# Moving the samples' state update of a state-space mixer to GpSimd, and the causal mask out of TensorE

## The chip, the cores and the metric

The kernel runs on one core of a Trainium2 chip. A core has five engines with instruction queues of their own: TensorE (PE in the profile; its weight loads are PEld), VectorE (DVE), ScalarE (ACT), GpSimd (POOL) and SyncE (SP), which only issues transfers here. The metric is device time in microseconds (us) of one execution of the whole program.

## The reference

One inference step of two layers with 1024 channels, for a prompt of 512 tokens and 8 samples of one token each. Layer 0 uses sparse attention, layer 1 a Mamba-2 mixer, and each is followed by an MLP. The change is in the mixer. For each of 32 heads with state `S` (64 x 128), cut to what matters:

```
xbc = silu(conv(h @ w_xbc));  x, B, C = split(xbc)           # B, C shared by the 8 heads of a group
a_cum  = cumsum(dt * a) within a chunk
decay  = exp(where(l >= s, a_cum[l] - a_cum[s], -1e30))       # causal
y      = ((C B^T) * decay) @ (x * dt)  +  exp(a_cum) * (C @ S_prev)  +  D * x      # prompt
S_new  = exp(dt * a) * S + (x * dt) B^T;   y = S_new C + D * x                     # each sample
out    = rmsnorm(y * silu(z)) @ w_out
```

The sequence result doesn't depend on the chunk length; the kernel uses chunks of 128.

## The kernel before

Activations lie as 128 channels by 520 columns: 512 prompt tokens, then 8 samples. Products with weights are exact to float32 by splitting both sides into a rounded high half and a remainder (float32r): ScalarE copies the high half of a weight tile (`split`, `wh`, line 408) and VectorE subtracts for the low half (line 409), two weights ahead of their product. A product of 128 output channels is 48 matmuls.

The mixer lies between about 890 and 1300 us. Four head groups of four pairs of heads each run through it, in the order of `SSD_SEQ` (line 1942): per pair q the x product of the next pair with its convolution (`ssd_x`), the pair itself (`ssd_pair`), then its z product and gate (`ssd_gate`). At a group's last pair the next group's B and C products come in (`ssd_bc`), at a group's first pair the output product of the group before (`ssd_out`). I call the two pairs of a group that have neither its plain pairs.

In a pair (`ssd_pair`), TensorE spreads the cumulated decay of the two heads over 128 partitions into PSUM (`ps`, line 1512) and adds the causal mask of 0 and -1e30 by a matmul with the identity (line 1514). ScalarE takes the exponential with a bias per chunk (line 1521) into `M`; VectorE multiplies by `cb`, the product of B and C (line 1522). A further spread through `sp` (a GpSimd copy, line 1525, and a matmul, line 1527) gives `E`. `xd` is x times its step, `st` the states from chunk to chunk, `y` the result. For the samples, in each pair, a loop over the 8 samples (lines 1577 to 1582) has ScalarE scale B by x (`xb`), VectorE update the state tile `ss` and VectorE multiply by C with a sum along the free axis (`ys`). The state, 128 x 1024 values, is loaded by SP and stored through GpSimd's queue.

A scheduler orders the instructions of each engine when the program is built, by its own estimate of when operands are ready; on the chip each engine takes its list in that order. So pieces of a pair stand between the matmuls of the neighbouring products. Tile pools set reuse: 4 PSUM tiles `s`, 2 of `M`, 2 of the state `ss`, 3 of `xb`, one `z`, one `y`.

## Time and profile before

| | before |
|---|---|
| median of three runs | 1721.11 us (1719.4 to 1721.38) |
| profiled execution | 1719.56 us, span 1717.9 us |
| PE busy | 1664.7 us (97%) |
| PEld busy | 1538.2 us (90%) |
| DVE busy | 984.0 us (57%) |
| ACT busy | 761.6 us (44%) |
| POOL busy | 143.5 us (8%) |
| mean granted TensorE clock | 0.993 |

The profiled execution's time is its span and what lies around it. Busy shares are means over stages with different limits, so the mixer is read by its own stretches below. Names of buffers come from the program with numbers left out: `a` is the PSUM tile of a product, `s` another PSUM tile, `c` any constant.

### The profile page before, as it was taken

Reading aid. Unit: us, or ns where it says so; the run is one execution under the profiler, and the core shown is the slowest. Engines: PE = TensorE matmul, PEld = TensorE weight load, DVE = VectorE, ACT = ScalarE, POOL = GpSimd, SP = SyncE. Lnnn points to the kernel's source line nnn. Section 1 sums busy time; section 2 is a strip of 40 time slices with the busy share of each in tenths; the row PEclk is TensorE's granted clock in tenths of the full one; section 3 lists DMA queues with packets and bytes.
Section 4 is the critical chain, followed back from the end, with each engine's and each line's share of the span. In section 5 each row is a group of like instructions: output and inputs, shape, how many; then the busy total and the mean of one; then the engine's idle time right before and its main releaser. Section 6 shows DMA issues by size and latency. Waiting matters only on the chain.

```text
span 1717.9 us, 34708 instructions
## 1 busy us (share of the span) xinstructions
PE 1664.7 (97%) x13878; PEld 1538.2 (90%) x13878; DVE 984.0 (57%) x2423; ACT 761.6 (44%) x1624; POOL 143.5 (8%) x303
## 2 busy tenths in 40 slices
PE   7899999999999999999999999999998999999997
PEld 6699877667989999999989898899987999999997
DVE  2543377776464343433478968879797643434344
ACT  3534366666443131322456666646564422323231
POOL 2000112310001000000001102111022000000000
PEclk9999999999999999999999999999999999999999
DMA  8822656545433523333433442344324232323321
GB/s 302 288 87 99 215 195 223 169 148 196 137 126 97 184 87 135 99 135 136 136 135 102 135 166 90 117 135 138 125 89 160 74 99 87 96 90 93 93 86 51
DMA packets 72114, 229.87 MB, mean 134 GB/s; under 512 B 8770, under 2 KB 15218, under 8 KB 71186
## 3 DMA queue, kind: packets, MB, share of 16 engines
q1 hardware_dynamic: 62546, 198.45, 35.1%
q0 software_dynamic: 8832, 28.16, 4.5%
q8 instruction: 109, 1.79, 0.4%
q10 hardware_dynamic: 576, 1.05, 0.2%
q14 instruction: 51, 0.42, 0.1%
HBM read 204.02 MB, written 23.61 MB: 133 GB/s over the span
## 4 chain that ended last, share of the span: by engine, by line
PE 71%; DVE 8%; ACT 2%; issue 1%; POOLq 0%; DMA 0%; SPq 0%; POOL 0%; DVEq 0%; ACTq 0%
PE a L323 60%; PE s L323 5%; PE f L323 2%; PE o L323 1%; DVE wh L336 1%; PE sc L323 1%; PE t L327 1%; DVE c L345 1%; DVE g L345 1%; ACT wh L330 1%; DVE acc L336 1%; PE s L327 0%; DVE ss L1462 0%; PE f L327 0%; ACT h L333 0%
## 5 line engine op out<-in xcount | busy, mean ns | idle before, releaser
L323 PE MATMUL a<-h,wh 128*128 128x256 f32 x5952 | 743.4, 284 | 3.8 <-ACT t L333 1.6
L323 PEld LDWEIGHTS a<-h,wh 128*128 128x128 f32 x5952 | 723.3, 189 | 10.1 <-issue 3.7
L330 ACT ACTIVATE wh<-w 128x1024 fp32r<-128x1024 f32 x212 | 224.5, 1059 | 521.8 <-PE a L323 480.4
L336 DVE TENSOR_TENSOR wh<-w,wh 128x1024 fp32r<-128x1024 f32 x212 | 259.6, 1225 | 266.4 <-ACT wh L330 265.8
L323 PEld LDWEIGHTS a<-hid,wh 128*128 128x128 f32 x3072 | 370.2, 188 | 5.0 <-issue 4.2
L323 PE MATMUL a<-hid,wh 128*128 128x256 f32 (+1 forms) x3072 | 373.7, 283 | 0.0
L336 DVE TENSOR_TENSOR t<-a,c 128x8 f32<-128x8 f32 x72 | 12.0, 167 | 217.4 <-PE a L323 217.4
L323 PE MATMUL a<-yh,wh 128*128 128x256 f32 (+1 forms) x768 | 98.4, 285 | 3.0 <-DVE acc L336 1.5
L323 PEld LDWEIGHTS a<-yh,wh 128*128 128x128 f32 x768 | 93.7, 188 | 5.2 <-DVE acc L336 2.2
L330 ACT ACTIVATE hid<-t 128x520 fp32r<-128x520 f32 x64 | 40.9, 639 | 84.5 <-DVE t L336 84.5
L330 ACT ACTIVATE h<-t 128x128 f32<-128x128 f32 (+3 forms) x128 | 52.5, 440 | 46.5 <-PE t L327 46.3
L333 ACT ACTIVATE h<-sc,m 128x128 f32<-128x128 f32 (+3 forms) x128 | 66.6, 530 | 14.6 <-DVE m L340 12.5
L336 DVE TENSOR_TENSOR hid<-t,hid 128x520 fp32r<-128x520 f32 x64 | 44.7, 700 | 42.3 <-ACT hid L330 42.3
L327 PE MATMUL t<-c,h 128*128 128x128 f32 x320 | 53.5, 281 | 1.9 <-DVE h L340 0.7
L345 DVE SCALAR_TENSOR_TENSOR c<-a,c,c 128x512 f32<-128x512 f32 (+1 forms) x74 | 53.9, 728 | 1.8 <-PE a L323 1.8
L333 ACT ACTIVATE xb<-bc,x 128x128 f32<-128x128 f32 x128 | 46.4, 419 | 15.8 <-DVE xb L345 11.2
L323 PE MATMUL sc<-kv,q 128*128 128x128 f32 (+3 forms) x128 | 49.5, 387 | 0.0
L323 PEld LDWEIGHTS a<-q,wh 128*128 128x128 f32 x384 | 46.3, 188 | 1.0 <-ACT wh L330 0.8
L327 PEld LDWEIGHTS t<-c,h 128*128 128x128 f32 x320 | 34.4, 141 | 13.8 <-issue 7.7
L323 PE MATMUL a<-q,wh 128*128 128x256 f32 (+1 forms) x384 | 46.7, 283 | 0.0
L323 PE MATMUL sc<-kv,c 128*128 128x128 f32 (+3 forms) x128 | 42.3, 331 | 4.2 <-POOL c L947 4.2
L1462 DVE SCALAR_TENSOR_TENSOR ss<-ss,c,xb 128x128 f32<-128x128 f32 x128 | 43.3, 361 | 4.4 <-ACT xb L333 4.2
(366 smaller groups left out, 1941.9 us busy)
## 6 DMA issues: line engine op xcount, KB each, us to landing
w<-in_w_dram SPq DMA_DIRECT2D x128, 512.0 KB, 3.5
w<-in_ada_w_dram SPq DMA_DIRECT2D x80, 512.0 KB, 3.6
w<-in_w_ssd_dram SPq DMA_DIRECT2D x40, 512.0 KB, 3.6
w<-in_w_nsa_dram SPq DMA_DIRECT2D x20, 512.0 KB, 3.6
ss<-in_ssm_dram SPq DMA_DIRECT2D x16, 512.0 KB, 4.3
out_ssm_s_dram<-ss POOLq DMA_DIRECT2D x16, 512.0 KB, 3.0
w<-in_w_sout_dram SPq DMA_DIRECT2D x16, 512.0 KB, 4.1
cm<-in_cmp_dram SPq DMA_DIRECT2D x24, 256.0 KB, 4.0
```

Source lines behind the costliest of these rows:

```text
L323: self.nc.tensor.matmul(out, lhsT, rhs, start=start, stop=stop, skip_group_check=True)
L327: self.nc.tensor.transpose(out, in_, self.C('ident')[0:k, 0:k])
L330: self.nc.scalar.activation(out, in_, AF.Copy, **kw)
L333: self.nc.scalar.activation(out, in_, f, **kw)
L336: self.nc.vector.tensor_tensor(out, a, b, op=op)
L345: self.nc.vector.scalar_tensor_tensor(out, a, s, b, op0=op0, op1=op1, **kw)
L1462: self.nc.vector.scalar_tensor_tensor(out, a, s, b, op0=op0, op1=op1)
```

## The change

The samples' update leaves the loop over samples: four GpSimd operations over 128 x 1024 values (state times decay, B times x, their sum, the result times C) in a function of their own, `ssd_sample`. It is issued behind the gate of the pair before (for the first pair, behind its x product), and the sum over the last axis is taken by VectorE in the gate. There is one `xb` buffer of 128 x 1024 in place of three of 128 x 128. The causal mask becomes a multiplication by 0 and 1 where B and C's product is copied (`cb`), now on VectorE. The exponent is limited to values of 0 and below by a Relu of the negated difference, four per head, followed by one exponential over 512 columns. `E` is taken from `ps` in two halves of 64 partitions, so `sp` and its matmul go. Two small operations of the convolution move from GpSimd to VectorE.

```diff
@@ dt_fin
-        self.ts(self.nac.rearrange(fl), p[:, 0:128], -1.0)
+        self.vcopy(self.ac.rearrange(fl), p[:, 0:128])
@@ conv
-        nc.gpsimd.memset(r[:, 0:3], 0.0)
+        nc.vector.memset(r[:, 0:3], 0.0)
...
-        nc.gpsimd.tensor_copy(self.CP[:, n, :], r[:, 512:515])
+        self.vcopy(self.CP[:, n, :], r[:, 512:515])
@@ ssd_bc
-        self.copy(cb, p)
+        self.tt(cb.rearrange("p (c l) -> p c l", c=4), p.rearrange("p (c l) -> p c l", c=4),
+                self.C('tri')[:, None, :].to_broadcast([128, 4, 128]), ALU.mult)
+    def ssd_sample(self, g, t, G):
+        q = 4 * g + t
+        xs, bc = G['xs'], G['bc']
+        v = self.ssd_state(q)
+        x8 = self.small([128, 8], 'x8', 2)
+        self.tt(x8, xs[:, 2 + t], self.sdb[:, q, 0, :], ALU.mult)
+        sh = [128, 8, 128]
+        x = self.tile('xb', sh)
+        f = self.nc.gpsimd.tensor_tensor
+        f(v, v, self.sdb[:, q, 1, :, None].to_broadcast(sh), op=ALU.mult)
+        f(x, bc[0], x8[:, :, None].to_broadcast(sh), op=ALU.mult)
+        f(v, v, x, op=ALU.add)
+        f(x, v, bc[1], op=ALU.mult)
+        self.store(self.O['ssm_s'][q], v.rearrange("p b n -> p (b n)"))
+        return x
@@ ssd_pair
-            self.mm(ps[e], self.e2R[r, 2 * q + e:2 * q + e + 1].to_broadcast([64, 128]), self.ac2[r], True, False)
-        for e in range(2):
-            self.mm(ps[e].rearrange("p (c l) -> p c l", c=4), self.identR,
-                    self.negsR[:, None, :].to_broadcast([128, 4, 128]), False, True)
+            self.mm(ps[e], self.e2R[r, 2 * q + e:2 * q + e + 1].to_broadcast([64, 128]), self.ac2[r], True, True)
...
-                self.act(m[:, ck(c)], p[:, ck(c)], AF.Exp, bias=self.nac[:, c, h:h + 1])
+                self.act(m[:, ck(c)], p[:, ck(c)], AF.Relu, scale=-1.0, bias=self.ac[:, c, h:h + 1])
+            self.act(m, m, AF.Exp, scale=-1.0)
             self.tt(m, m, cb, ALU.mult)
...
-        sp = self.tile('sp', [64, 2, 64], F32R)
-        self.nc.gpsimd.tensor_copy(sp, self.e2R[0:64, 2 * q:2 * q + 2, None].to_broadcast([64, 2, 64]))
-        p = self.tile('s', [128, 512])
-        self.mm(p[:, 128:512], sp.rearrange("p a b -> p (a b)"), self.ac2[0:64, 128:512], True, True)
         E = self.tile('E', [128, 512])
-        self.act(E[:, 128:512], p[:, 128:512], AF.Exp)
+        for e in range(2):
+            r = slice(64 * e, 64 * e + 64)
+            self.act(E[r, 128:512], ps[e][r, 128:512], AF.Exp)
...
-        for b in range(8):
-            v = w[:, b]
-            x = self.tile('xb', [128, 128])
-            self.act(x, bc[0][:, b], AF.Copy, scale=x8[:, b:b + 1])
-            self.pool_stt(v, v, self.sdb[:, q, 1, b:b + 1], x, ALU.mult, ALU.add)
-            self.stt(x, v, 1.0, bc[1][:, b], ALU.mult, ALU.mult, accum_out=ys[:, b:b + 1])
@@ ssd_gate, behind the z product
+        ys = self.small([128, 8], 'ys', 2)
+        self.nc.vector.tensor_reduce(ys, yn, AX.X, ALU.add)
+        self.stt(y[:, 512:T], xs[:, 2 + t], self.dsk[:, q:q + 1], ys, ALU.mult, ALU.add)
@@ ssd
             elif kind == 'z':
-                self.ssd_gate(g, t, y)
+                self.ssd_gate(g, t, y, G[g]['xs'], Y)
+                if n < 15:
+                    Y = self.ssd_sample((n + 1) // 4, (n + 1) % 4, G[(n + 1) // 4])
```

(`pool_stt` runs on VectorE in spite of its name.) What the scheduler makes of it on GpSimd, in the third group between the additions into `yss` of two plain pairs; `z` and `yss` are the gate's, `cv` is the convolution's input. Before:

```order
L1602 TENSOR_TENSOR yss_11760<-yss_11760,z_14826 128x520
L1525 COPY sp_15106<-c_7410 64x128
L1442 COPY c_7409<-cv_14891 128x3
L1439 MEMSET cv_15327 128x3
L357 DMA out_ssm_p_dram<-st_14958 128x128
L357 DMA out_ssm_s_dram<-ss_14911 128x1024
L1525 COPY sp_15605<-c_7410 64x128
L1602 TENSOR_TENSOR yss_11760<-yss_11760,z_15076 128x520
```

After, the same place:

```order
L1604 TENSOR_TENSOR yss_11728<-yss_11728,z_14533 128x520
L1510 TENSOR_TENSOR ss_15159<-ss_15159,c_11317 128x1024
L1511 TENSOR_TENSOR xb_14768<-bc_13722,x_14766 128x1024
L1512 TENSOR_TENSOR ss_14764<-ss_14764,xb_14768 128x1024
L1513 TENSOR_TENSOR xb_14768<-ss_14764,bc_13722 128x1024
L356 DMA out_ssm_p_dram<-st_14670 128x128
L356 DMA out_ssm_s_dram<-ss_14764 128x1024
L1604 TENSOR_TENSOR yss_11728<-yss_11728,z_14754 128x520
```

Four 128x1024 operations stand where two small copies and a memset stood; the decay product (`ss_15159`) is already that of the pair behind the one whose chain follows it.

VectorE at the same place, before: the end of a pair, with pieces of the samples' loop (`xb`, `ss`) between its steps.

```order
L345 SCALAR_TENSOR_TENSOR xb_15011,ys_14986<-ss_14911,bc_13960 128x128
L336 TENSOR_TENSOR y_14980<-y_14980,E_14935 128x384
L1462 SCALAR_TENSOR_TENSOR ss_14911<-ss_14911,c_11320,xb_15015 128x128
L336 TENSOR_TENSOR x_15159<-xs_13790,c_11320 128x8
L336 TENSOR_TENSOR wh_15200<-w_14771,wh_15199 128x1024
L345 SCALAR_TENSOR_TENSOR xb_15015,ys_14986<-ss_14911,bc_13960 128x128
L345 SCALAR_TENSOR_TENSOR z_15076<-z_15076,a_15027 128x520
L345 SCALAR_TENSOR_TENSOR y_14980<-xs_13790,c_7390,ys_14986 128x8
L336 TENSOR_TENSOR M_15094<-M_15094,g_13946 128x512
L336 TENSOR_TENSOR y_14980<-y_14980,z_15076 128x520
L336 TENSOR_TENSOR M_15100<-M_15100,g_13946 128x512
```

VectorE after, from behind the small product `x_14766` (`x8`) on which GpSimd's `xb_14768` waits, to the sum over it:

```order
L344 SCALAR_TENSOR_TENSOR st_14670<-st_14670,c_99,s_14665 128x64 x6
L344 SCALAR_TENSOR_TENSOR y_14692<-x_14392,c_7387,s_14679 128x512
L335 TENSOR_TENSOR E_14646<-E_14646,s_14688 128x384
L344 SCALAR_TENSOR_TENSOR z_14754<-z_14754,a_14702 128x520
L335 TENSOR_TENSOR y_14692<-y_14692,E_14646 128x384
L335 TENSOR_TENSOR M_14778<-M_14778,g_13708 128x512
L335 TENSOR_TENSOR y_14692<-y_14692,z_14754 128x520
L335 TENSOR_TENSOR xd_14800<-s_14795,c_99 128x512
L335 TENSOR_TENSOR M_14785<-M_14785,g_13708 128x512
L335 TENSOR_TENSOR wh_14846<-w_14475,wh_14845 128x1024
L344 SCALAR_TENSOR_TENSOR yh_14761<-y_14692,c_7384,yh_14760 128x520
L1591 TENSOR_REDUCE ys_15146<-xb_14768 128x8
```

The samples' pieces are gone, and the reduction stands behind GpSimd's chain of the same pair.

## Rows read from the trace of the kernel before

**Rows 1.** Stretches: length; busy PE, PEld, DVE, ACT, POOL; clock; DMA share; GB/s
```profile
1098.74:1142.04 43.30, 42.38 (x339) 39.49 (x339) 32.58 (x91) 23.33 (x65) 3.82 (x8) 1.00 0.39 124
1142.04:1156.45 14.41, 14.41 (x129) 14.12 (x128) 12.85 (x34) 7.24 (x15) 2.74 (x5) 1.00 0.29 86
1156.45:1174.64 18.19, 18.03 (x137) 15.37 (x136) 17.27 (x47) 14.40 (x44) 4.81 (x7) 1.00 0.35 107
1174.64:1203.70 29.06, 28.83 (x247) 28.06 (x246) 25.00 (x71) 16.20 (x36) 3.96 (x9) 1.00 0.47 153
```
**Rows 2.** The same stretches, samples' instructions alone: DVE, ACT busy
```profile
1098.74:1142.04 43.30, 8.69 (x48) 5.79 (x16) 1.00 0.39 124
1142.04:1156.45 14.41, 1.85 (x9) 1.38 (x4) 1.00 0.29 86
1156.45:1174.64 18.19, 3.84 (x16) 2.66 (x7) 1.00 0.35 107
1174.64:1203.70 29.06, 5.17 (x24) 1.78 (x5) 1.00 0.47 153
```
**Rows 3.** Waits of PE, 890 to 1310 us: total, times, longest
```profile
PE a L323 <- DVE acc L336: 1.5, 3, 0.6
```
**Rows 4.** PE in order of time, a pair's masks: start, us
```profile
1157.76 1.16 PE L323 MATMUL s<-c,c 64*128 64x512 f32 x4
1158.85 0.43 PE L323 MATMUL s<-c,sp 64*128 64x384 f32 x1
1159.22 0.66 PE L327 MATMUL s<-c,x 128*128 128x128 f32 x4
```
**Rows 5.** POOL: one line (ns: least/median/largest), then in order of time
```profile
L1602 POOL TENSOR_TENSOR yss<-yss,z x14: 1289/1311/1572, 950.5 to 1279.8; 128x520 f32<-128x520 f32 x14
1101.80 0.28 POOL L1525 CAST sp<-c 64x128 fp32r<-64x128 f32 x1 [1.74 <-PE s L323]
```
**Rows 6.** POOL and DVE in order of time, where they meet
```profile
1159.79 1.21 DVE L336 TENSOR_TENSOR wh<-w,wh 128x1024 fp32r<-128x1024 f32 x1
1159.89 1.16 POOL L1442 COPY c<-cv 128x3 f32<-128x3 f32 x1 [0.17 <-ACT cv L330]
...
1308.58 1.49 POOL L534 TENSOR_TENSOR st<-st,M 128x520 f32<-128x520 f32 x1 [2.13 <-ACT M L333]
1308.82 1.28 DVE L336 TENSOR_TENSOR us<-c,A 128x8 f32<-128x8 f32 x1
1312.10 0.16 DVE L336 TENSOR_TENSOR us<-c,A 128x8 f32<-128x8 f32 x1
```
**Rows 7.** DVE by time, then by line (busy, mean ns), mixer
```profile
1177.97 1.23 DVE L345 SCALAR_TENSOR_TENSOR st<-st,c,s 128x64 f32<-128x64 f32 x6
1179.12 0.74 DVE L345 SCALAR_TENSOR_TENSOR y<-x,c,s 128x512 f32<-128x512 f32 x1
1179.78 0.55 DVE L336 TENSOR_TENSOR E<-E,s 128x384 f32<-128x384 f32 x1
...
L345 DVE SCALAR_TENSOR_TENSOR z<-z,a 128x520 f32<-128x520 f32 x16 | 11.0, 690 | 0.6 <-ACT z L333 0.6
L336 DVE TENSOR_TENSOR y<-y,E 128x384 f32<-128x384 f32 x16 | 8.8, 553 | 0.0
```
**Rows 8.** DVE by line, mixer and the stretch behind it
```profile
L336 DVE TENSOR_TENSOR wh<-w,wh 128x1024 fp32r<-128x1024 f32 x53 | 64.7, 1221 | 28.9 <-ACT wh L330 28.5
...
L495 DVE TENSOR_REDUCE c<-s 128x36 f32<-128x144 f32 x1 | 0.3, 307 | 0.2 <-PE s L327 0.2
```
**Rows 9.** ACT by line, mixer
```profile
L333 ACT ACTIVATE xb<-bc,x 128x128 f32<-128x128 f32 x128 | 46.4, 419 | 15.8 <-DVE xb L345 11.2 <-DVE x L336 3.9 <-DMA bc<-dr 0.5
L333 ACT ACTIVATE th<-x 128x512 f32<-128x512 f32 x16 | 10.3, 642 | 12.2 <-DVE x L345 12.1
```
**Rows 10.** Stretches behind the mixer, columns as in rows 1
```profile
1320.00:1325.00 5.00, 0.95 (x6) 0.29 (x3) 4.93 (x10) 1.90 (x5) 3.08 (x2) 0.99 0.99 391
1325.00:1330.00 5.00, 4.42 (x21) 4.33 (x22) 0.28 (x2) 2.16 (x4) 0.00 (x0) 0.50 0.06 24
```

More of the change, by code (lines that the diff above doesn't have):

```diff
@@ L47, in shape_constants @@
     put('tri', (i[:, None] <= i[None, :]).astype(np.float32))
-    put('negs', np.where(i[:, None] <= i[None, :], 0.0, NEG))
     t = np.arange(4)[None, :, None] * 128 + i[:, None, None]
@@ L1407, in dt_fin @@
         m = self.m[0].rearrange("p a b -> p (a b)")
-        self.nac, self.cd, self.dtde = (m[:, ck(n)].rearrange("p (c h) -> p c h", c=4) for n in range(3))
+        self.ac, self.cd, self.dtde = (m[:, ck(n)].rearrange("p (c h) -> p c h", c=4) for n in range(3))
         fl = "p c h -> p (c h)"
-        self.ts(self.nac.rearrange(fl), p[:, 0:128], -1.0)
+        self.vcopy(self.ac.rearrange(fl), p[:, 0:128])
         self.copy(ae, p[:, 128:256])
@@ L1501, in ssd_state, with ssd_pair @@
         return w
-    def ssd_pair(self, g, t, X, G, w):
+    def ssd_sample(self, g, t, G):
         q = 4 * g + t
-        C, cb, bt, xs, bc = (G[k] for k in ('C', 'cb', 'bt', 'xs', 'bc'))
+        xs, bc = G['xs'], G['bc']
[11 more added lines that the diff above has]
+        return x
+    def ssd_pair(self, g, t, X, G):
+        q = 4 * g + t
+        C, cb, bt, xs = (G[k] for k in ('C', 'cb', 'bt', 'xs'))
         M = []
@@ L1572, in ssd_pair, with ssd_gate @@
         self.tt(y[:, 128:512], y[:, 128:512], E[:, 128:512], ALU.add)
-        x8 = self.small([128, 8], 'x8', 2)
-        self.tt(x8, xs[:, 2 + t], self.sdb[:, q, 0, :], ALU.mult)
-        ys = self.small([128, 8], 'ys', 2)
-        for b in range(8):
-            v = w[:, b]
-            x = self.tile('xb', [128, 128])
-            self.act(x, bc[0][:, b], AF.Copy, scale=x8[:, b:b + 1])
-            self.pool_stt(v, v, self.sdb[:, q, 1, b:b + 1], x, ALU.mult, ALU.add)
-            self.stt(x, v, 1.0, bc[1][:, b], ALU.mult, ALU.mult, accum_out=ys[:, b:b + 1])
-        self.store(self.O['ssm_s'][q], w.rearrange("p b n -> p (b n)"))
-        self.stt(y[:, 512:T], xs[:, 2 + t], self.dsk[:, q:q + 1], ys, ALU.mult, ALU.add)
         return y
-    def ssd_gate(self, g, t, y):
+    def ssd_gate(self, g, t, y, xs, yn):
         q = 4 * g + t
         ps = self.product(('w_ssd', 10 * g + 3 + 2 * t), self.h)
+        ys = self.small([128, 8], 'ys', 2)
+        self.nc.vector.tensor_reduce(ys, yn, AX.X, ALU.add)
+        self.stt(y[:, 512:T], xs[:, 2 + t], self.dsk[:, q:q + 1], ys, ALU.mult, ALU.add)
         z = self.U('z')
```

13 lines of the change are left out of this document (6 added, 7 removed).

## The prediction

> **What bounds the kernel now.** I read four views in turn. First the busy time by stretch, cut at the ends of the pairs of one head group in the mixer [rows 1]. Each stretch runs from one addition into `yss` (end of a gate) to the next. In the two plain pairs (14.41 and 18.19 us, one x and one z product each) TensorE is busy throughout: 14.41 and 18.03 us. So TensorE sets the pace. VectorE is close behind: 12.85 of 14.41, then 17.27 of 18.19 us. In the pair that also makes the next B and C (29.06 us) and in the one that also runs the output product (43.30 us) VectorE has 4 and 11 us free. Second, the same stretches for the samples' work alone [rows 2]: 1.85 and 3.84 us of VectorE in the plain pairs, 5.17 and 8.69 us in the others. The scheduler has put most of that work where VectorE has room. Third, TensorE's waits [rows 3]: the largest sum in the whole mixer is 1.5 us, for VectorE. Fourth, the POOL and DVE rows in order of time [rows 6], for what happens when the two engines meet; the sum hangs on it.
>
> **TensorE.** Per pair the change takes away two mask matmuls and the `sp` matmul. The four 512-column matmuls start at 1157.76 and the `sp` matmul at 1158.85 [rows 4]: 1.09 us, 0.27 each, so 0.54 for two. The next matmuls start 0.37 us after `sp`. Together 0.91 us a pair, 14.6 us for 16 pairs. TensorE is the bound, so this is gained wherever it stays the bound.
>
> **ScalarE.** It loses eight scalings of `xb` a pair (0.42 us each) and gains two exponentials of 512 columns (the 512-column Tanh, 0.64, is the nearest row) and a second half of `E` [rows 9]. It gets lighter, and it is busy 7.24 of 14.41 and 14.40 of 18.19 us in the plain pairs [rows 1], so this hides. The first masked product comes 0.64 us later in a pair; between nothing and 16 times that, 10 us, I take nothing, because in [rows 1] ScalarE's and VectorE's other work decides when that product starts.
>
> **VectorE's own work.** The samples' part [rows 2] goes. What is left of the two plain pairs is 30.12 less 5.69, 24.43 us, 12.2 each. A sum over 1024 elements is added: a reduction of 144 elements took 0.31 and a 1024-column subtraction 1.22 us [rows 8]; between them I take 1.2, since the second has the size. The small memset and copy that leave POOL cost some 0.2. So 13.6 us a plain pair, against 16.3 on average before: free of POOL, VectorE would be well off the path.
>
> **What a POOL operation costs.** Four per pair, 128x1024. The nearest row is the 128x520 addition, 1.31 us (least 1.29) [rows 5]. In proportion that is 2.6 us; with a fixed part of some 0.2 (all of the one-input cast of 128 elements is 0.28 [rows 5]), 2.4. Below stands that cast, whose 0.1 us beyond the fixed part would give about 1.0 for 1024 elements. I take 2.4, by the addition, which is the same operation. The Trainium skill (GPSIMD Engine Reference, section 3.1, Elementwise) gives 4497 ns for 2048 elements; an estimate from it is 2.25 us here, and with it the forecast below would be 1743.
>
> **Where the two meet.** At 1308.58 POOL starts an addition that ends at 1310.07. A VectorE product of only 8 columns, issued at 1308.82, ends at 1310.10: 1.28 us, where the same form alone takes 0.16. The other way round, POOL's copy of three elements takes 1.16 us when a 1.21 us VectorE subtraction runs [rows 6]. So a VectorE instruction with both inputs in SBUF and a POOL instruction that reads SBUF exclude each other for their whole length. Before, POOL ran one such addition a pair. Now it runs five.
>
> I follow one plain pair in the changed order of VectorE with these lengths. The decay product on POOL stands behind `yss`; VectorE's next two-input instruction is at its door at once and waits 2.4. The product `xb` starts behind VectorE's small `x8`; VectorE now has six `st` steps, `y`, `E` and `z`, each with one input in PSUM: 1.15, 0.66, 0.47 and some 0.65 us, 2.9 in all [rows 7], so nothing is lost. `y` plus `E` is ready 2.9 us in, the second POOL operation ends at 4.8: wait 1.9. It runs 0.5 [rows 7], POOL's third operation takes the port, and the product M waits 2.4 behind it. Sum 6.7 us a pair; I take 6.6 because something of the first wait is over by the time VectorE comes. The bounds are 0 (all four under one-input work or idle time) and 9.6 (four times 2.4). The Trainium skill (SBUF — State Buffer, "Who interferes with whom") lets an instruction with one SBUF input and a reduction pass beside POOL; no row here shows one that starts inside a POOL operation, and if they waited too, the upper bound would hold, about 1771.
>
> **The sum, against the profiled execution's 1719.6 (span 1717.9 and 1.7 around it).** Plain pair: 13.6 + 6.6 = 20.2 us of VectorE, against 15.4 (16.3 less 0.9) of TensorE. VectorE is in order, prepares the low half of every weight and the M, `xd` and `st` that TensorE takes a few tenths later, so TensorE waits: 20.2 - 16.3 = +3.9 us. There are eight such pairs: +31.2. The pair with B and C: 19.8 (25.00 less 5.17), 1.2, 0.6 for the memsets and copies, 0.7 for the mask product, 6.6: 28.9 us against 29.06 before, -0.2, three times. The pair with the output product: 23.9 + 8 is far below 43, so TensorE's 0.9 is gained, three times: -2.7. First and last pair: -1.8. Sum 31.2 - 0.6 - 2.7 - 1.8 = +26 us, 1745.7. The median of the runs shown is 1.5 above the profiled time, so 1747.
>
> The state's load moves ahead on SP (0.3 us to issue); it needs the buffer of two pairs ago, whose store stands directly behind that pair's last POOL operation, a pair earlier, so it does not hold the weights behind it. On POOL the store of `ssm_p` and `yss` now stand behind up to four long operations; their readers are a pair away.
>
> **Rivals.**
> - *Hidden.* POOL's operations cost VectorE only idle or one-input time (or cost 1.0 us each: the walk then loses 2.0, and 15.6 us is TensorE's own pace). Then only TensorE's saving is left: 1721.1 - 14.6 = 1706.5. For it: VectorE loses 19.6 us of its own work in each group (the four of [rows 2]), more than the 16 us or so of waits that I add outside the first operation of a pair. Against it: [rows 6], and two plain pairs a group with 3 us of room.
> - *Half hidden.* Half of the 6.6: 16.9 against 16.3, +0.6 in eight pairs, less 6: about 1720.
> - *Every wait reaches TensorE.* In the other pairs too TensorE takes M, `xd` and `st` the moment they exist, and a 2.4 us wait there is not caught up by later room. 64 operations at 1.65 less 14.6: +91, 1812. It decides if TensorE comes to each of the pair's matmuls with no product matmuls left to put ahead of them. Against it: in those pairs VectorE has 4 and 11 us free [rows 1], and there it can be ahead with the weights.
> - *The clock.* After 1320 to 1325, with TensorE busy 0.95 of 5 us, the granted clock was 0.50, the lower level, for the next five [rows 10]. If the waits in the plain pairs open a gap like that, a quarter of 8 times 15.4 us at the lower level adds 31: 1778. In the forecast single waits stay at 2.4 us, so I think it less likely.
>
> **How the numbers follow.** Forecast 0.50 (own range 1730 to 1768), hidden 0.25, half hidden 0.06, every wait 0.12, clock 0.07. The measurement tells apart about 0.2% (3.4 us): faster 0.25, same 0.06, slower 0.69. The range reaches from the hidden case to beyond the clock's, 1705 to 1790; what it leaves is most of "every wait" and the lower edge of "hidden".
>
> **What would show it.** Right: POOL's 128x1024 operations at 2.4 us or above, 64 of them; the mean of `y` plus `E` and of M well above their 0.55 and 0.68 us; plain pairs from `yss` to `yss` near 20 us; TensorE's waits on `wh`, M or `xd` of VectorE summing to some 30 us or more. Wrong: plain pairs near 15.4 us with few waits (hidden), POOL's operations near 1 us, or granted clock below 1.00 inside the mixer. The one term that could sink the forecast is the 6.6 us: should VectorE run into POOL only while it had nothing urgent, the sign turns.

## The result and the profile after

The changed kernel takes 1775.5 us (median of four runs, 1766.1 to 1782.2) against 1721.2 (four runs, 1719.4 to 1729.0): ratio 1.0303, 95% interval 1.0245 to 1.0360. The forecast was 1747. It is slower, as forecast, by about twice the amount. The profiled execution, the fastest of the four, took 1766.1 us (span 1764.5, granted clock 0.980) against 1719.6, +46.6.

First the busy time of the group that [rows 1] shows: the pair with the output product, two plain pairs, the pair with B and C.

```profile
1121.63:1168.39 46.76, 42.12 (x319) 40.31 (x318) 31.63 (x45) 17.24 (x40) 20.67 (x13) 0.93 0.32 107
1168.39:1188.65 20.26, 20.21 (x166) 18.73 (x165) 15.38 (x30) 11.78 (x28) 10.59 (x6) 1.00 0.23 75
1188.65:1208.39 19.74, 16.07 (x107) 13.59 (x106) 17.36 (x33) 13.57 (x40) 10.95 (x8) 0.91 0.30 106
1208.39:1238.58 30.19, 29.94 (x247) 28.39 (x246) 24.69 (x57) 14.90 (x30) 6.96 (x5) 1.00 0.44 145
```

The group took 116.95 us against 104.96. TensorE now stands still in the first and third pair, and the clock, 1.00 before in all four, is below it in just those. Over the whole program: the first addition into `yss` comes 12.7 us later than before, the stretch of the 14 additions is 362.2 us instead of 329.3 (+32.9), the rest +0.9. By kind of pair, against before: seven plain pairs +18.4, three with the output product +11.2, three with B and C +3.3.

TensorE's waits, the answer to [rows 3] (total, times, longest):

```profile
PE s L322 <- DVE xd L335: 23.6, 8, 4.9
PE a L322 <- DVE acc L335: 5.1, 2, 2.6
PE s L322 <- DVE M L335: 2.2, 2, 1.6
```

Next POOL's and VectorE's groups by line (busy, mean ns, idle before and its ends), the answer to [rows 5, 7, 8]:

```profile
L1512 POOL TENSOR_TENSOR ss<-ss,xb 128x1024 f32<-128x1024 f32 x16 | 43.6, 2728 | 1.0
L1513 POOL TENSOR_TENSOR xb<-ss,bc 128x1024 f32<-128x1024 f32 x16 | 41.6, 2600 | 1.2
L1511 POOL TENSOR_TENSOR xb<-bc,x 128x1024 f32<-128x1024 f32 x16 | 32.0, 2001 | 74.5 <-DMA bc<-dr 45.4 <-DVE x L335 26.1 <-DVE ys L1591 1.8
L1510 POOL TENSOR_TENSOR ss<-ss,c 128x1024 f32<-128x1024 f32 x16 | 30.9, 1934 | 88.3 <-DMA ss<-in_ssm_dram 63.9 <-ACT c L329 24.4
...
L335 DVE TENSOR_TENSOR wh<-w,wh 128x1024 fp32r<-128x1024 f32 x52 | 79.7, 1533 | 27.6 <-ACT wh L329 27.5
L1591 DVE TENSOR_REDUCE ys<-xb 128x8 f32<-128x1024 f32 x16 | 19.4, 1211 | 16.1 <-POOL xb L1513 16.1
L335 DVE TENSOR_TENSOR y<-y,E 128x384 f32<-128x384 f32 x15 | 17.5, 1165 | 0.0
L347 DVE COPY c<-cv 128x3 f32<-128x3 f32 x24 | 11.9, 495 | 0.0
L344 DVE SCALAR_TENSOR_TENSOR z<-z,a 128x520 f32<-128x520 f32 x15 | 10.3, 689 | 0.1
```

`wh` (1221 before) and `y` plus `E` (553) are longer, `z`, with one input in PSUM, is not (690). I call the four operations of a pair its chain. Two entries were in no part of the forecast: the reduction waits 16.1 us for POOL's last operation, and POOL's second operation waits 45.4 us for the transfer of B and C. It also waits 26.1 us for VectorE's `x8` (`x` in the row), which the forecast had early. So a chain that is issued a pair ahead does not run a whole pair ahead.

In order of time, all in the group above: the head of the pair with the output product (1119.69 to 1127.38), its middle (to 1150.92), and behind the last "..." the end of the first plain pair:

```profile
1119.69 1.98 POOL L1511 TENSOR_TENSOR xb<-bc,x 128x1024 f32<-128x1024 f32 x1 [20.27 <-DMA bc<-dr]
...
1123.35 3.36 POOL L1512 TENSOR_TENSOR ss<-ss,xb 128x1024 f32<-128x1024 f32 x1
1124.48 2.26 DVE L347 COPY c<-cv 128x3 f32<-128x3 f32 x1
1126.65 0.68 DVE L335 TENSOR_TENSOR xd<-s,c 128x512 f32<-128x512 f32 x1
1127.38 1.72 PE L322 MATMUL s<-xd,g 128*128 128x128 f32 x8 [2.01 <-DVE xd L335]
...
1140.89 1.89 POOL L1511 TENSOR_TENSOR xb<-bc,x 128x1024 f32<-128x1024 f32 x1 [2.69 <-DVE x L335]
1145.67 3.24 POOL L1513 TENSOR_TENSOR xb<-ss,bc 128x1024 f32<-128x1024 f32 x1
1148.95 1.22 DVE L1591 TENSOR_REDUCE ys<-xb 128x8 f32<-128x1024 f32 x1 [2.27 <-POOL xb L1513]
1150.92 1.45 PE L322 MATMUL a<-yh,wh 128*128 128x256 f32 x8 [2.60 <-DVE acc L335]
...
1179.54 0.16 DVE L335 TENSOR_TENSOR x<-xs,c 128x8 f32<-128x8 f32 x1
1179.80 2.18 POOL L1511 TENSOR_TENSOR xb<-bc,x 128x1024 f32<-128x1024 f32 x1 [0.80 <-DVE x L335]
1185.38 2.73 POOL L1513 TENSOR_TENSOR xb<-ss,bc 128x1024 f32<-128x1024 f32 x1
1188.15 1.22 DVE L1591 TENSOR_REDUCE ys<-xb 128x8 f32<-128x1024 f32 x1 [2.28 <-POOL xb L1513]
1191.98 0.68 DVE L335 TENSOR_TENSOR xd<-s,c 128x512 f32<-128x512 f32 x1
1192.72 1.01 PE L322 MATMUL s<-xd,g 128*128 128x128 f32 x3 [3.56 <-DVE xd L335]
```

The group's first chain is held back by B and C, so its tail falls on the head of the pair with the output product; there it holds a three-column copy and with it `xd` and TensorE. The second chain goes on only at 1140.89, 11.7 us behind the end of the first, when VectorE has come to its `x8`; its reduction, already in VectorE's list ahead of the output product's additions, waits for it, and TensorE waits for those. In the plain pair the third chain goes on only at 1179.80, when VectorE has come to `x8`, which stands behind the six `st` steps and `E` there; it ends at 1188.1, the reduction is late, and so are the gate, `xd` behind it, and TensorE by 3.56 us. The order of VectorE shown ahead of the prediction is that of the second plain pair, where `x8` stands ahead of the `st` steps and the reduction does not wait.

Behind most such gaps the clock falls: between 880 and 1330 us TensorE has nine gaps of 2.0 to 4.9 us, and the granted clock drops to 0.50, the lower of its two levels, for some us, during or behind eight of them. Stretches around the gap that ends at 1150.92:

```profile
1148.50:1151.00 2.50, 0.08 (x1) 0.12 (x2) 2.05 (x3) 0.68 (x1) 0.94 (x2) 1.00 0.81 328
1151.00:1153.50 2.50, 2.50 (x15) 2.50 (x16) 1.51 (x2) 0.00 (x0) 0.00 (x0) 0.64 0.28 87
1153.50:1156.00 2.50, 2.50 (x16) 2.50 (x16) 0.38 (x1) 0.00 (x0) 0.28 (x1) 0.68 0.89 311
```

TensorE, busy 0.08 of 2.5 us, is granted 0.64 and 0.68 on average in the next five, though it is busy throughout: 1.7 us of full-speed time not granted.

### The profile page after: what moved, and what is told of

It is laid out like the page before. It is cut to its first block, busy times and chain, and to the rows that moved or that the text cites. A ratio compares the mean times of both kernels' runs of the same rounds, so it can differ in the third digit from the quotient of the medians.

```text
span 1764.5 us, 34107 instructions
## 1 busy us (share of the span) xinstructions
PE 1680.1 (95%) x13830; PEld 1551.3 (88%) x13830; DVE 996.6 (56%) x2106; ACT 746.7 (42%) x1540; POOL 271.6 (15%) x302
## 4 chain that ended last, share of the span: by engine, by line
PE 64%; DVE 11%; ACT 3%; issue 2%; POOL 2%; SPq 1%; POOLq 0%; DMA 0%; DVEq 0%; ACTq 0%
PE a L322 55%; PE s L322 3%; DVE wh L335 2%; PE f L322 1%; PE o L322 1%; DVE x L344 1%; PE sc L322 1%; DVE y L335 1%; PE t L326 1%; DVE c L344 1%; POOL ss L1512 1%; POOL xb L1513 1%; DVE acc L335 1%; ACT wh L329 1%; DVE c L347 1%
## 5 line engine op out<-in xcount | busy, mean ns | idle before, releaser
L322 PE MATMUL a<-h,wh 128*128 128x256 f32 x5952 | 757.4, 286 | 3.9 <-ACT t L332 1.6
L322 PEld LDWEIGHTS a<-h,wh 128*128 128x128 f32 x5952 | 730.9, 190 | 15.9 <-issue 9.2
L335 DVE TENSOR_TENSOR wh<-w,wh 128x1024 fp32r<-128x1024 f32 x212 | 275.7, 1301 | 266.8 <-ACT wh L329 265.1
L322 PE MATMUL a<-yh,wh 128*128 128x256 f32 (+1 forms) x768 | 105.5, 296 | 6.2 <-DVE acc L335 5.1
L322 PEld LDWEIGHTS a<-yh,wh 128*128 128x128 f32 x768 | 99.7, 199 | 9.8 <-issue 8.4
L332 ACT ACTIVATE h<-sc,m 128x128 f32<-128x128 f32 (+3 forms) x128 | 66.6, 530 | 14.5 <-DVE m L339 12.4
L322 PE MATMUL a<-q,wh 128*128 128x256 f32 (+1 forms) x384 | 46.5, 283 | 0.0
L344 DVE SCALAR_TENSOR_TENSOR x<-cv,c,x 128x512 f32<-128x512 f32 x48 | 45.8, 954 | 0.0
```

Of the source, the lines that this page charges most:

```text
L322: self.nc.tensor.matmul(out, lhsT, rhs, start=start, stop=stop, skip_group_check=True)
L332: self.nc.scalar.activation(out, in_, f, **kw)
L335: self.nc.vector.tensor_tensor(out, a, b, op=op)
L344: self.nc.vector.scalar_tensor_tensor(out, a, s, b, op0=op0, op1=op1, **kw)
```

## The experiments

Each time is the ratio to the kernel before, run on the same chip, with its 95% interval. Every edit changes operand times, so the scheduler also writes the lists anew; no run here changes an instruction and leaves all else in place.

**Without POOL's operations.** The state is stored and summed as loaded (the samples' update is left out):

```diff
-        f(v, v, self.sdb[:, q, 1, :, None].to_broadcast(sh), op=ALU.mult)
...
-        f(x, v, bc[1], op=ALU.mult)
-        return x
+        return v
```

> The changed kernel without POOL's four operations a pair (it leaves out the samples' state update: the state is stored as it was loaded and the reduction is taken over it). Everything else of the change stays: order, masks, reduction, copies on VectorE. Theory 1 (POOL's operations and the waits they cause are the whole loss): TensorE's saving is left, about 1705 us, clock 1.00 in the mixer, plain pairs near 15.4 us. Rival 2 (order, Relu under the exponential, or the wait of the reduction cost the time): 1740 to 1775.

0.9954 (0.9922 to 0.9985). The four operations, with the waits for them, are all of the loss: 1.0303 to 0.9954 is 60 us by the medians, 52 by the profiled spans (1764.5 and 1712.2). But only about 8 us of the 14.6 that TensorE saves come out (3 to 13 by the interval), and the plain pairs last 18.06 and 17.02 us, not the 15.4 expected. The first three pairs of the same group:

```profile
1093.54:1134.19 40.65, 40.05 (x327) 37.93 (x326) 24.73 (x43) 15.88 (x35) 2.43 (x4) 1.00 0.34 105
1134.19:1152.25 18.06, 17.46 (x137) 15.35 (x136) 14.48 (x31) 11.63 (x31) 2.40 (x4) 1.00 0.34 113
1152.25:1169.27 17.02, 17.02 (x136) 15.26 (x135) 15.37 (x34) 15.73 (x43) 2.41 (x4) 1.00 0.38 128
```

**The same operations with results that nobody reads** (update left out):

```diff
-        f(v, v, self.sdb[:, q, 1, :, None].to_broadcast(sh), op=ALU.mult)
+        f(x, v, self.sdb[:, q, 1, :, None].to_broadcast(sh), op=ALU.mult)
...
-        return x
+        return v
```

> The changed kernel with the same four POOL operations of the same sizes and operands in SBUF, but their results go to a scratch tile that nobody reads: the reduction is taken over the state as loaded, and the state is stored as loaded (the samples' update is left out of the result). So POOL is as busy as in the changed kernel, and no instruction of VectorE depends on it through these data. Theory 1 (the engines exclude each other at SBUF): the loss stays, 1762 to 1776, at most 8 to 10 us less, for the waits of the reduction on POOL ahead of the additions of the output product (2.3 to 2.6 us, three times) and in the start. Rival (VectorE waits in order for POOL's chain of four, a plain dependency): about 1714, as without POOL's operations.

1.0382 (1.0313 to 1.0451): in its trace no VectorE instruction waits for POOL's results, and it is no faster than the change (14 us slower by the ratios, the intervals overlap). So exclusion alone is enough for the loss. That nothing was gained where the waits of the reduction went, 8 to 10 us by the expectation, is a miss; VectorE's busy time rose by another 25 us (table below), since the operations now meet other instructions. The same run shows what passes: a reduction inside a POOL operation.

```profile
933.67 2.23 POOL L1511 TENSOR_TENSOR xb<-bc,x 128x1024 f32<-128x1024 f32 x1
934.07 1.21 DVE L1591 TENSOR_REDUCE ys<-ss 128x8 f32<-128x1024 f32 x1
```

**Eight halves instead of four operations:**

```diff
-        f(v, v, self.sdb[:, q, 1, :, None].to_broadcast(sh), op=ALU.mult)
+        hs = [slice(0, 4), slice(4, 8)]
+        sh = [128, 4, 128]
+        for s in hs:
+            f(v[:, s], v[:, s], self.sdb[:, q, 1, s, None].to_broadcast(sh), op=ALU.mult)
...
```

> The changed kernel, but each of POOL's four 128x1024 operations in two halves of 128x512, eight a pair. POOL's own time goes up by a fixed part each (some 0.2 us, four times a pair). If the price is set by the total time that POOL holds VectorE (theory 1): the sum of both engines' work is unchanged or some 0.8 us a pair longer, so 1775 to 1788. If it is set by the length of a single wait, with the gaps of TensorE of over 2 us and the clock that falls behind them (theory 1b): the single waits fall to about 1.2 us, VectorE gets in between, the granted clock of the mixer returns towards 1.00 (0.96 in the changed kernel) and the time falls to 1745 to 1765.

1.0314 (1.0253 to 1.0375), and 0.95 of clock in the mixer: halving POOL's operations brings nothing. VectorE was indeed held up 18 us less than in the changed kernel, but its reductions now waited 36.5 us for POOL instead of 16.1.

**The three-column copy on ScalarE, and a reduction of nothing** (the second leaves out the sum over the state):

```diff
-        self.vcopy(self.CP[:, n, :], r[:, 512:515])
+        self.copy(self.CP[:, n, :], r[:, 512:515])
```

> The changed kernel, but the 128x3 copy out of `cv` goes to ScalarE instead of VectorE (the memset stays on VectorE). The trace of the changed kernel shows this copy at 0.5 us on average and up to 2.3 us beside POOL's long operations, directly ahead of the `xd` product that TensorE then waits for 2 to 5 us. Theory 1a (this copy is one of the mis-sized terms): VectorE is freed of 24 times 0.5 us and TensorE of some of its waits on `xd`, so 5 to 15 us less than the changed kernel, 1760 to 1770. Rival (it only stands in front of the same wait: the next instruction with both inputs in SBUF meets the same POOL operation): no difference that can be measured from the changed kernel, 1775.

1.0263 (1.0206 to 1.0319): 7 us less by the ratios, between the two expectations, and the intervals overlap, so the time does not decide. The profile speaks for the rival: without the 24 copies (11.9 us) VectorE is busy 355.3 us from 880 us to the last addition into `yss`, with them 354.7, so other instructions were held up in their place.

```diff
-        self.nc.vector.tensor_reduce(ys, yn, AX.X, ALU.add)
+        self.vcopy(ys, yn[:, :, 0])
```

> The changed kernel with the reduction over 1024 elements replaced by a copy of eight of them (the sum over a sample's state is left out): the dependency on POOL's chain stays, VectorE's 1.2 us a pair go. Theory 1 with VectorE as the bound in the plain pairs: 1.1 us in each of seven plain pairs and about as much in the start, 8 to 12 us less than the changed kernel, about 1763 to 1767. Rival (the price lies in where VectorE meets POOL, not in how much it has to do): within 4 us of the changed kernel, 1772 to 1779.

1.0218 (1.0156 to 1.0279): 15 us less than the change by the ratios, for 16 times 1.1 us less of VectorE's work. It suggests that the price lies also in how much VectorE has to do, almost one for one; the intervals overlap a little, so it is not shown.

**Which chains?** Chains left out by pair (their update is left out), five runs; in place of `q < 2` the others have `q >= 4 and t in (0, 1)`, then `(2, 3)`, `(0,)` and `(1,)`:

```diff
+        if q < 2:
+            self.store(self.O['ssm_s'][q], v.rearrange("p b n -> p (b n)"))
+            return v
```

> The changed kernel without POOL's four operations for samples of the first two pairs only (their state is stored as it was loaded). In the changed kernel the first pair ends 12.7 us later than before, where -0.9 was forecast; two chains of four operations run there one behind the other. Theory 1c (this start is a mis-sized term of its own): 10 to 15 us less than the changed kernel, 1760 to 1766, and the rest of the mixer unchanged. Rival (the start is late for another reason, the later first M or the state's load): less than 4 us gained.

1.0178 (1.0107 to 1.0249): by the ratios 22 us less, more than the 10 to 15 expected; the profiled span is 16.4 us shorter, 14.5 of it before the first addition into `yss`.

> The changed kernel without POOL's four operations for the first and second pair of head groups 2 to 4 (6 of 16 pairs; their samples' state is stored as loaded, so the samples' update of those pairs is left out). In the trace of the changed kernel these two chains run, but for the tail of the second and the head of the first, inside the pair that also has the output product. The reading of the traces so far: that pair carries as much of the loss as the plain ones (46.7 us against 40.7 without any POOL operation), so 15 to 20 us less than the changed kernel, about 1757. The prediction as it stood (that pair has 11 us of VectorE free and hides everything): no more than 3 us less, 1772 to 1776.

1.0118 (1.0068 to 1.0167): 32 us less, twice what I expected.

> The changed kernel without POOL's four operations for the third and fourth pair of head groups 2 to 4 (6 of 16 pairs; their samples' update is left out). Their chains run, but for one operation, inside the two plain pairs. The prediction as it stood (all of the loss is in the plain pairs, +3.9 us over before in each, 4.8 over TensorE's own time): 6 times 4.8, some 27 to 30 us less than the changed kernel, about 1747. The reading of the traces so far (plain pairs 2.2 and 2.7 us longer than without POOL's operations, some of it given back in the next pair): 10 to 15 us less, about 1762.

1.0257 (1.0207 to 1.0307): 8 us, not to be told from the change. So leaving out the chains that run in the plain pairs, on which the forecast stood, gains next to nothing. That is a net result: in the profile the plain pairs of the group are 3.0 and 1.7 us shorter (17.28 and 18.05 us), but the pair with the output product is 3.4 longer (50.16), and reductions wait 8.2 us for POOL in it (2.3 in the change). What these chains cost by themselves is better seen from the run with five left out below.

> The changed kernel without POOL's four operations for the first pair of head groups 2 to 4 (3 of 16 pairs; their samples' update is left out). This chain is held back by the transfer of B and C and runs at the head of the pair with the output product, where TensorE waits 2.0 us for `xd`. If the first chain carries the loss of that pair: most of the 31 us that both chains gave, 1745 to 1755. If it is the second chain: 1765 to 1775. If either alone is enough to spoil the pair: both runs gain less than 10 us.

1.0091 (1.0054 to 1.0127): leaving out the three first chains of groups 2 to 4 gives 36 us by the ratios, all that both had given and more than I expected (24 by the profiled spans). The group then, 106.74 us:

```profile
1116.70:1157.32 40.62, 39.74 (x326) 37.85 (x325) 27.08 (x43) 15.83 (x35) 10.92 (x7) 1.00 0.33 105
1157.32:1176.40 19.08, 18.75 (x149) 16.68 (x148) 15.88 (x31) 11.64 (x31) 9.08 (x7) 1.00 0.22 76
1176.40:1194.25 17.85, 16.48 (x127) 14.30 (x125) 15.20 (x33) 15.96 (x43) 9.62 (x8) 1.00 0.44 144
1194.25:1223.44 29.19, 28.10 (x238) 27.13 (x237) 26.89 (x57) 14.54 (x30) 5.61 (x4) 1.00 0.50 162
```

> The changed kernel without POOL's four operations for the second pair of head groups 2 to 4 (3 of 16 pairs; their samples' update is left out). This chain runs in the middle of the pair with the output product; the reduction of the first pair and the additions of the output product stand behind its operations on VectorE, and TensorE waits 2.6 us for the additions. If the second chain carries the loss: 1745 to 1755; if the first: 1765 to 1775; if either alone is enough: both gain less than 10 us.

1.0237 (1.0184 to 1.0289): 11 us, and the interval overlaps with the change's. So the loss of this pair goes with the first chain, which spoils its own pair's head. But VectorE's list differs too. With the first chain left out, the `x8` of the second stands 9.2 us into the pair with the output product, ahead of the `st` steps (1125.88 us); in the changed kernel it stands 19.0 us into it, behind them (1140.64), and in the first plain pair it moves likewise (9.1 against 11.2). How much of the gain is the chain and how much the new order, no run here separates.

**Five at once** (the update of the first two pairs of the mixer and of the first pair of groups 2 to 4 is left out):

```diff
+        if q in (0, 1, 4, 8, 12):
+            self.store(self.O['ssm_s'][q], v.rearrange("p b n -> p (b n)"))
+            return v
```

> The changed kernel without POOL's four operations for five of the 16 pairs: the first two of the mixer and the first of head groups 2 to 4 (their samples' update is left out); eleven chains run as in the changed kernel. If these five carry the loss and the other eleven fit beside VectorE's work: as without any POOL operation, or a little above, 1713 to 1727 on the scale of before at 1721. If the eleven others have a price as the prediction gave the plain pairs (3.9 us and more each in seven pairs): 1740 or above.

1.0009 (0.9980 to 1.0039), clock 1.00 through the mixer. By the ratios five chains cost 51 us and the other eleven about 9; by the profiled spans 40 and 12. In the plain pair of this run that begins at 1140.10 the chain goes on 9.3 us into the pair (11.4 in the changed kernel, 1179.80 above), is through in 6.9 us (8.3), and the reduction does not wait. Here too `x8` has moved ahead of the `st` steps:

```profile
1149.17 0.17 DVE L335 TENSOR_TENSOR x<-xs,c 128x8 f32<-128x8 f32 x1
1149.41 1.90 POOL L1514 TENSOR_TENSOR xb<-bc,x 128x1024 f32<-128x1024 f32 x1 [8.00 <-DVE x L335]
1150.40 1.24 DVE L344 SCALAR_TENSOR_TENSOR st<-st,c,s 128x64 f32<-128x64 f32 x6 [1.06 <-ACT st L329]
1151.39 2.40 POOL L1515 TENSOR_TENSOR ss<-ss,xb 128x1024 f32<-128x1024 f32 x1
1153.86 2.40 POOL L1516 TENSOR_TENSOR xb<-ss,bc 128x1024 f32<-128x1024 f32 x1
1154.35 2.33 DVE L335 TENSOR_TENSOR y<-y,E 128x384 f32<-128x384 f32 x1
1158.35 1.21 DVE L1594 TENSOR_REDUCE ys<-xb 128x8 f32<-128x1024 f32 x1
```

One of the three operations meets an instruction with two inputs in SBUF (2.33 instead of 0.55 us).

**The five done as before, eleven on POOL** (the result is kept):

```diff
+        w = self.ssd_state(q) if q in (0, 1, 4, 8, 12) else None
...
+        if w is not None:
+            for b in range(8):
+                self.act(x, bc[0][:, b], AF.Copy, scale=x8[:, b:b + 1])
```

> The changed kernel with the samples' update of those five pairs done as before (ScalarE scales, VectorE updates, inside the pair) and of the other eleven on POOL a pair ahead; the result is kept. If the five carry the loss and the work put back finds room as it did before: 1716 to 1728, no different from before. If VectorE's work put back into the pair with the output product and the start costs what it did not cost before (0.6 us of it a pair came to 10 us in the run with one head's clamp): 1735 to 1750.

1.0209 (1.0136 to 1.0282). A miss: the eleven chains are those of the run before, and yet reductions wait 12.4 us for POOL again and TensorE 23.6 us for `xd`. In the first plain pair of the group, which begins at 1165.23:

```profile
1174.33 0.16 DVE L335 TENSOR_TENSOR x<-xs,c 128x8 f32<-128x8 f32 x1
1182.59 1.22 DVE L1607 TENSOR_REDUCE ys<-xb 128x8 f32<-128x1024 f32 x1 [4.14 <-POOL xb L1515]
```

`x8` comes as early as in the run before (9.1 us into the pair), but it stands behind the `st` steps and `E` again, and the reduction stands directly behind `z`, so VectorE has little left to do while the chain runs. Why the order comes out so is not shown.

**The mask part alone, in four versions.** First as it is in the change, the samples' loop as before:

```diff
-            self.act(m[:, ck(c)], p[:, ck(c)], AF.Exp, bias=self.nac[:, c, h:h + 1])
+            self.act(m[:, ck(c)], p[:, ck(c)], AF.Relu, scale=-1.0, bias=self.ac[:, c, h:h + 1])
+        self.act(m, m, AF.Exp, scale=-1.0)
```

> Only the mask part of the change: the causal mask as a product with B.C, Relu under the exponential, E taken from the two heads' own rows, so per pair two 512-column mask matmuls and the `sp` matmul gone; the samples' update stays on VectorE and ScalarE inside the pair and the three-column copies stay on POOL, as before. Theory 1 (the loss of the change is POOL's and VectorE's mutual exclusion alone): TensorE's 0.91 us a pair is gained, 16 times, so about 1706 us, and the granted clock in the mixer stays at 1.00. Rival 2 (the longer chain to the first M, Relu then Exp then product, is what makes TensorE wait in the changed kernel): no gain, or slower than before, 1721 to 1760. Rival 3 (TensorE's saving only turns into waits on VectorE, which is close behind in the plain pairs): about 1713 to 1721.

1.0008 (0.9974 to 1.0042): no gain, Rival 2 or 3. TensorE's matmuls did go, as these rows of before and of this run show for 14 pairs (23.1 to 9.5 us, 0.97 a pair):

```profile
L323 PE MATMUL s<-c,c 64*128 64x512 f32 (+1 forms) x56 | 17.0, 473 | 0.0
L323 PE MATMUL s<-c,sp 64*128 64x384 f32 x14 | 6.1, 436 | 0.0
```

```profile
L322 PE MATMUL s<-c,c 64*128 64x512 f32 x28 | 9.5, 496 | 0.0
```

The same run's ScalarE by line:

```profile
L332 ACT ACTIVATE M<-M 128x512 f32<-128x512 f32 x28 | 17.9, 639 | 0.0
L332 ACT ACTIVATE E<-s 64x384 f32<-64x384 f32 x28 | 13.7, 489 | 0.3
```

Twice 0.64 a pair for the new exponential and twice 0.49 for `E` where one of 0.54 stood: ScalarE has 1.7 us a pair more.

One exponential, no Relu (the decay inside a chunk is left out):

```diff
-                self.act(m[:, ck(c)], p[:, ck(c)], AF.Relu, scale=-1.0, bias=self.ac[:, c, h:h + 1])
-            self.act(m, m, AF.Exp, scale=-1.0)
+                self.act(m[:, ck(c)], p[:, ck(c)], AF.Exp, scale=1e-6, bias=self.ac[:, c, h:h + 1])
```

> The mask part alone (as in the first run of this study) with the two steps of Relu and exponential made one: four exponentials with a bias of a scaled input per head, no 512-column exponential behind them (the decay inside a chunk is left out of the result). Theory A (the 14.6 us of TensorE's matmuls were lost because ScalarE got 1.3 us a pair more and the first M comes later): the saving appears, 1706 to 1712. Theory B (the saving goes into TensorE's waits for VectorE, `xd` and the additions, which set the pace a little behind it): as the mask part alone, 1718 to 1727.

0.9939 (0.9914 to 0.9965): 10.5 us of the 14.6. Theory A: the two exponentials on ScalarE held the saving back, by their load or by the longer way to M; this run takes away both. Then the clamp on VectorE, for one head and for both (the result is kept):

```diff
+                self.ts(m[:, ck(c)], p[:, ck(c)], self.ac[:, c, h:h + 1], 0.0, ALU.subtract, ALU.min)
```

> The mask part alone, with the clamp of the first head's exponents moved from ScalarE (four Relu of 0.38 us) to VectorE (four subtract-and-min steps that read PSUM, some 0.2 us each); the second head's stay on ScalarE. The result is kept. If ScalarE's way to M is what held the saving back: ScalarE loses 1.5 us a pair and VectorE gains 0.8, so part of the 10 us that one exponential gave, 1711 to 1718. If VectorE is as near the bound as ScalarE: no gain, 1718 to 1726.

> As the run before with the clamp of both heads on VectorE: ScalarE loses 3 us a pair against the mask part alone, VectorE gains 1.7. If ScalarE's way to M alone decides: 1706 to 1714, the fastest. If VectorE, at 274 of 328 us in the mixer before this, becomes what TensorE waits for: 1720 to 1735.

1.0057 (1.0028 to 1.0086) and 1.0161 (1.0121 to 1.0201), both above what either expectation allowed. The second is clearly slower than with Relu on ScalarE; the first's interval overlaps with that run's. A step took 0.34 us, not 0.2, so VectorE got 1.2 and 2.4 us a pair more, 19 and 39 in all; the time rose by 8 and 26 us although ScalarE lost as much (its 38.6 us of Relu became 19.0, then none). So VectorE's load weighs more than ScalarE's. The way to M is hardly shorter in these two (four steps of 0.34 us in place of 0.38), so they say nothing of its length.

**The mask part with the eight scalings on POOL** in one operation a pair (the result is kept):

```diff
-            self.act(x, bc[0][:, b], AF.Copy, scale=x8[:, b:b + 1])
+        nc.gpsimd.tensor_tensor(xs8, bc[0], x8[:, :, None].to_broadcast([128, 8, 128]), op=ALU.mult)
```

> The mask part alone, and of the samples' update only the eight scalings of `xb` a pair moved from ScalarE to one broadcast multiplication of 128x1024 on POOL; state update and products with C stay on VectorE inside the pair. One long POOL operation a pair instead of four. If the loss goes with POOL's time beside VectorE (1.9 of the 9 us of the four, 52 us in all): some 11 us above the mask part alone, 1732 to 1738, less what ScalarE's 3.4 us a pair give back. If ScalarE's load was what held the mask part's saving back, and one operation finds room between VectorE's one-input work: 1708 to 1716, and the fastest of all.

1.0143 (1.0096 to 1.0189), 23 us above the mask part alone, twice the price by POOL's time: the state update now waits for POOL too (14.8 us in eight waits).

**The samples' part alone,** masks by matmul as before:

```diff
-            self.mm(ps[e], self.e2R[r, 2 * q + e:2 * q + e + 1].to_broadcast([64, 128]), self.ac2[r], True, True)
+            self.mm(ps[e], self.e2R[r, 2 * q + e:2 * q + e + 1].to_broadcast([64, 128]), self.ac2[r], True, False)
...
-                self.act(m[:, ck(c)], p[:, ck(c)], AF.Relu, scale=-1.0, bias=self.ac[:, c, h:h + 1])
+                self.act(m[:, ck(c)], p[:, ck(c)], AF.Exp, bias=self.nac[:, c, h:h + 1])
...
+        self.nc.gpsimd.tensor_copy(sp, self.e2R[0:64, 2 * q:2 * q + 2, None].to_broadcast([64, 2, 64]))
```

> The other part of the change alone: the samples' update on POOL a pair ahead and the small columns on VectorE; masks by matmul, `sp` matmul and direct exponential as before. If the two parts add up as in the prediction (TensorE's saving of 14.6 us is there and hidden under nothing), this is 14.6 us above the changed kernel, about 1787 to 1790. If the mask part is worth what it was worth alone (nothing, 1.0008), this equals the changed kernel, 1770 to 1777. If VectorE is the bound in the plain pairs, the mask matmuls hide there and the truth is between, 1776 to 1784.

1.0500 (1.0435 to 1.0564), above all three expectations. The two parts do not add: the mask part is worth nothing alone and 34 us here. The reductions wait 46.1 us for POOL in this run (16.1 in the change). Why the lists come out so much worse stays open.

No version tried that keeps the result is faster than the kernel before; the mask part alone equals it.

**The runs together.** These are the nine runs in which VectorE's own work is that of the changed kernel. VectorE's lateness, worked out from each profile: its busy time from 880 us to the last addition into `yss`, less 301.5 us in the run without POOL's operations; and its reductions' waits for POOL. Beside it what the span is above that run's 1712.2; numbers in brackets are pairs of groups 2 to 4:

| run | busy more | waits for POOL | sum | span more |
|---|---|---|---|---|
| five chains left out | 24.1 | 0 | 24.1 | 12.2 |
| (0, 1) left out | 32.4 | 0 | 32.4 | 21.6 |
| (0) left out | 41.4 | 0 | 41.4 | 28.6 |
| (1) left out | 41.9 | 4.6 | 46.5 | 42.9 |
| first two left out | 34.7 | 16.1 | 50.8 | 35.9 |
| (2, 3) left out | 38.4 | 22.2 | 60.6 | 46.4 |
| changed kernel | 53.1 | 16.1 | 69.2 | 52.3 |
| halves | 34.9 | 36.5 | 71.4 | 60.7 |
| results apart | 78.5 | 0 | 78.5 | 74.1 |

Beyond some 4 to 17 us, each microsecond by which VectorE is late, by exclusion or by waiting, comes out in the time, what the clock adds included. It fits the halves (one form for the other) and the apart run (all of one form). It is a relation over nine runs, not a separate proof for each.

## Why the prediction was right and wrong

Right: the direction and the cause. POOL's and VectorE's operations exclude each other, at full length, by the forms named: `y` plus `E`, M and `wh` are long beside POOL, a one-input `z` is not. POOL's operations took 1.93 to 2.73 us on average (forecast 2.4), the reduction 1.21 (1.2). TensorE's waits on VectorE sum to 30.9 us in the three rows above (some 30), the plain pairs of the group last 20.26 and 19.74 us (20.2); but that last agreement is luck, as the terms below show.

Term by term against before: the seven plain pairs behind the first addition into `yss` took 18.4 us more where 27.3 stood, the three pairs with the output product 11.2 more where 2.7 less stood, the three with B and C 3.3 more (0.6 less), the start with its one plain pair 12.7 more (3.0 more), the end 0.9 more (0.9 less). So the miss lies in the output pairs and the start, while the plain pairs cost less than forecast.

The step that failed is the place: "The pair with the output product: 23.9 + 8 is far below 43, so TensorE's 0.9 is gained, three times". I let room in a pair, read from a share of busy time, absorb the waits there, as if VectorE could do its urgent work elsewhere in the pair. These pairs lost 3.7 us each instead of gaining 0.9, and leaving out the first chain of three groups alone, with the new order that comes with it, gives back 36 us: of the 12.0 that the group above lost it returns 10.2, 6.1 in its own pair, 3.1 in the two plain ones (20.26 to 19.08, 19.74 to 17.85) and 1.0 in the last. VectorE's list is in order and TensorE's matmuls come at fixed places in theirs; a chain at the head of that pair makes `xd` late however idle VectorE is at its end. The rival that every wait reaches TensorE named this, and I gave it 0.12.

The terms, as the runs size them:
- Plain pair, exclusion 6.6 us: VectorE's instructions in the two plain pairs of the group took 2.2 and 3.1 us longer than the same forms did (by their median) in the run without POOL's operations; in the pair with the output product it was 5.6, from 880 us to the first addition 18.7. With the three first chains left out, plain pairs last 19.08 and 17.85 us, against 18.06 and 17.02 without POOL. The 20.2 of the forecast came out by another composition: VectorE was busy 15.38 and 17.36 us, not 20.2; the rest is the reduction's wait for a late chain and the gap and clock behind it. I had put the second operation behind an early `x8`. That holds for the second plain pair only: in the first one of groups 3 and 4 `x8` stands 11.2 us into the pair. In group 2 it stands ahead of the `st` steps there, 9.1 us in, and that pair lasts 19.07 us.
- The walk behind the 6.6 mixed two starts: 4.8 counts from the start of POOL's first operation, 2.9 from the end of VectorE's first wait. By one clock `y` plus `E` is ready at 5.3 and meets the third operation, not the second. The sum of 6.7 is the same by luck.
- First and last pair, -1.8: the start costs +12.7, and 14.5 come back with its two chains left out. I had not followed the first two chains, which stand back to back behind the late B and C.
- TensorE's saving, 14.6: the matmuls went (0.97 a pair, forecast 0.91), but the mask part alone gains nothing, with one exponential 10.5. For ScalarE's way to M I took nothing out of nothing to 10 us; taking away the added exponentials brought 10.5, the upper end.
- VectorE's own work in a plain pair, 13.6: 14.48 and 15.37 in the run without POOL's operations.
- The small copy "some 0.2" a pair: 0.50 on average, up to 2.3 beside POOL, but it stands in front of an instruction that would wait as long.
- The clock, held less likely because "single waits stay at 2.4 us": waits reached 4.9, and the granted clock is 0.96 in the 83 us of the start and the 362 us behind it. That is at most 18 us of full-speed time (0.04 of both) of the 46.6 that this execution lost. How much of it would have been a wait otherwise, no run isolates.
- The state's load, said not to hold the weights behind it: SP's queue waits 100.8 us for stores of the state in the mixer (45.5 before), but no engine waits for a weight there, so this is not a cause.

The Trainium skill (SBUF — State Buffer, "Who interferes with whom") holds that a reduction never contends with GpSimd on this chip and that a copy can, if its operands meet certain conditions. The trace agrees on both: 1.21 us inside a POOL operation above, and 0.16 us against 1.95 to 2.26 for the four of 24 copies that met one. So the upper bound that I had put on its being wrong, 1771, is not why the time came out there. The forecast took 2.4 us an operation and named 2.25 as an estimate from the Trainium skill (GPSIMD Engine Reference, section 3.1, Elementwise). Measured, operations that met no VectorE instruction took 1.9 us with a broadcast operand and 2.4 with two full ones.

## What to carry over

Room in a stretch is not room at the place where work is put: follow each new long operation to the moment it can start (its last operand, here `x8` and a transfer), in every kind of pair, and name what stands behind it in an in-order list there. When two engines are both near the bound, size a saving on one by taking away work on the other: here one to three us of VectorE or ScalarE a pair decided whether TensorE's 0.9 us showed. And test a part where it stands in the whole, since parts that share an order do not add. When an edit lets the scheduler write the lists anew, compare the lists before giving the gain to the edit.

## What was not expected of the hardware

A copy of three fp32 columns from SBUF to SBUF on VectorE, 0.16 us alone, is held for 2.26 by a POOL operation, as long as a two-input product. And the granted clock falls behind gaps of TensorE of 2.0 to 4.9 us in this kernel, where I had expected single waits of 2.4 us to leave it alone. Yet of two gaps of 2.0 us in pairs of the same kind, the one that ends at 1127.38 is followed by 0.50 and the one that ends at 1244.31 is not (1.00 to 1250), so the gap's length alone does not tell.
